# Two-layer hybrid block: residual tiles loaded ahead of the mixer-result tiles in both output projections

## The chip, the cores and the metric

The kernel runs on one core of a Trainium2 chip. The metric is the time of one execution in microseconds (us), measured on the device; lower is better. TensorE (PE) multiplies matrices, VectorE (DVE), ScalarE (ACT) and GpSimd (POOL) do elementwise work, and every DMA of this kernel is issued by SyncE (SP), whose queue issues them one after the other in the order of the program.

## The reference

Two layers of a block that runs three mixers side by side on 1024 positions of width 1024, with 256 context positions beside them. The first layer needs the context's output too, the second does not. Cut to what matters here:

```python
def hybrid_layer(x, ctx, ...):
    h  = rms_norm(x) * (1 + scale) + shift          # and hc from ctx
    ... = split_columns(h @ w_in, IN_SPLITS)
    attn_lat = attn_out(diff_attention_blocked(...), ag)
    ssd_lat  = ssd_out(ys_l, xs_l, z)               # chunked scan, both directions
    ret_lat  = ret_out(yr_l, rg)                    # retention, both directions
    mix   = concatenate([attn_lat, ssd_lat, ret_lat], axis=-1)   # 2048 wide
    x_new = x + gate * (mix @ w_out)
    ...
    ctx_new = ctx + gate_c * (mix_c @ w_out)
```

The change touches only how `mix @ w_out` and the sum with `x` are fed.

## The kernel before

Activations lie transposed, features on the 128 partitions and positions along the rows. The positions are cut into three chunks: c0 (0 to 511), c1 (512 to 1023) and c2 (the 256 of the context). Each float32 matrix product is made of three products of rounded halves: a tile `ah` and its remainder `al`, a weight `wh` and its remainder `wl`; ACT makes the rounded half, DVE or POOL the remainder (line 284).

The mixers write their results to an HBM buffer `mix` of 16 tiles of 128 features. The product with `w_out` is done in two parts. `out1` takes the eight tiles of the scan mixer as soon as those are there, adds gate times product to the residual `x` and stores the sum as `x1`; `out2` takes the other eight tiles and adds to `x1`. In both, `load_mix` brings a chunk's eight tiles by DMA (`mr`, line 1201); in `out1` DVE scales them (line 1205) before they are split. Then `out1` goes through four weight blocks of two output tiles each (`ci` 0 to 3) and, in each, through the chunks. A finished group of matmuls lies in one of two PSUM buffers. `evac` empties it: a DMA brings the residual tile `xr` (line 1221, from `in_xt` in the first layer, from `xl` in the second), DVE multiplies the PSUM tile by the gate and adds it to `xr` (line 1223), and a DMA stores the sum (line 1225). PE can begin the third group from now only when line 1223 has emptied the buffer of the first.

The tiles `mr` and `xr`, and many others, come from one pool `work` of eight buffers of 128x512 float32. A DMA into a `work` tile waits until the tile's former owner is done with it, and because the SP queue is in order, everything behind that DMA waits too.

Nobody writes the order of the instructions by hand. The code yields pieces of several such streams, and a scheduler then lays each engine's instructions out by its own estimate of times, so that retention pieces (rotations at lines 924 to 929, `ks` and `qs` at lines 1141 and 1167, `rs` at 1156, the finish of a head at lines 1090 and 1099) stand between those of `out1` on each engine. `raw` (line 270) are weight tiles. In the first layer `out2` also loads the `x1` tiles `xn` (line 469), which line 1292 updates.

Of the kernel before, what the change touches and what calls it, by code (L numbers as in the profile page):

```python
# [26 lines left out]
CHUNKS = ((0, 512), (512, 512), (1024, 256))  # L27
# [20 lines left out]
def drain(g):  # L48
    for _ in g:
        pass  # L50


class Net:
# [1156 lines left out]
    def out1(self, l, last, cols, xin):  # L1210
        nc = self.nc
        cs = (0, 1) if last else (0, 1, 2)
        for c in cs:
            self.load_mix(c, range(4, 12), cols, True)
            yield 0.5
        ada = self.ada_t[l]
        for ci in range(4):
            def evac(ft, t0, n, ps):
                f = 2 * ci + ft
                x = self.keep_x(f, t0, n) if self.mixed else self.work("xr")[:, 0:n]  # L1220
                nc.sync.dma_start(out=x, in_=xin[f, :, t0:t0 + n])
                gc = ada[:, 16 + f, 0 if t0 < LAT else 1:][:, 0:1]
                nc.vector.scalar_tensor_tensor(out=x, in0=ps, scalar=gc, in1=x, op0=ALU.mult, op1=ALU.add)  # L1223
                if not self.mixed:
                    nc.sync.dma_start(out=self.x1[f, :, t0:t0 + n], in_=x)

            w = self.next_w()
            for c in cs:
                t0, n = CHUNKS[c]
                for ft in range(2):  # L1230
                    if self.mixed and ci > 1 and len(self.wu) < 2:
                        self.stage_u(l)
                    evac(ft, t0, n, self.t_group(w, ft, c))
                    yield n * 24 / 2400
# [15 lines left out]
    def out2(self, l, last, cols, xout):  # L1250
        nc = self.nc
        while self.pieces:
            self.pieces.pop(0)()
        cs = (0, 1) if last else ORDER
        ada = self.ada_t[l]
        ws = []
        for ci in range(2):
            hi, lo = self.next_w(ci == 0)
            for ft in range(2):
                f = slice(ft * P, ft * P + P)  # L1260
                ws.append(([hi[:, k, f] for k in range(KT)], [lo[:, k, f] for k in range(KT)]))
        for pc in range(4):
            if len(self.wu) <= pc:
                self.stage_u(l)
        for hi, lo in self.wu:
            ws.append(([hi[:, k, :] for k in range(KT)], [lo[:, k, :] for k in range(KT)]))
        self.wu = []
        self.x1t = {}
        xs = {}
        for c in cs:  # L1270
            self.load_mix(c, (0, 1, 2, 3, 12, 13, 14, 15), cols, False)
            if not last:
                xs[c] = self.load_x(c, self.x1, "xn2")
        for c in cs:
            if c == cs[-1]:
                self.prefetch()
            t0, n = CHUNKS[c]
            ah, al = self.act[c]
            acc = self.work("acc") if not last else None
            for f in range(KT):  # L1280
                ps = self.pmm()
                self.mm3(ps[:, 0:n], ws[f][0], ws[f][1], [ah[:, k, :] for k in range(KT)],
                         [al[:, k, :] for k in range(KT)], True)
                if last:
                    x = self.x1k.pop((t0, f), None)
                    if x is None:
                        x = self.work("xr")[:, 0:n]
                        nc.sync.dma_start(out=x, in_=self.x1[f, :, t0:t0 + n])
                else:
                    x = xs[c][f]  # L1290
                gc = ada[:, 16 + f, 0 if c < 2 else 1:][:, 0:1]
                nc.vector.scalar_tensor_tensor(out=x, in0=ps[:, 0:n], scalar=gc, in1=x, op0=ALU.mult, op1=ALU.add)
                nc.sync.dma_start(out=xout[f, :, t0:t0 + n], in_=x)
                if not last:
                    self.sumsq_add(acc, x, f, n)
                    if c == cs[-1] and f == 3:
                        self.load_dt(l + 1)
                        self.layer_params(l + 1)
            if not last:
                def post(c=c, xs=xs[c], acc=acc):  # L1300
                    return self.norm_h(l + 1, c, xs, self.norm_r(c, acc))

                if c != cs[-1]:
                    drain(post())
                else:
                    self.posts = {0: post}
# [247 lines left out]
```

## Time and profile before

| | us |
|---|---|
| median of 3 runs | 2867.38 (2867.06 to 2869.82) |
| the profiled execution's own time | 2869.1 |
| its span, first to last instruction | 2867.3 |
| PE busy | 2665.5 (93%) |
| DVE busy | 1781.3 (62%) |
| ACT busy | 1056.4 (37%) |
| POOL busy | 772.1 (27%) |

The profiled execution is 1.7 us above the median, 1.8 us of its time lie outside the span, and PE is busy for nearly all of it. Times below are microseconds from the span's start.

### The profile page before, as it was taken

Reading aid. Unit: us, or ns where it says so; the run is one execution under the profiler, and the core shown is the slowest. Engines: PE = TensorE matmul, PEld = TensorE weight load, DVE = VectorE, ACT = ScalarE, POOL = GpSimd, SP = SyncE. Lnnn points to the kernel's source line nnn. Section 1 sums busy time; section 2 is a strip of 40 time slices with the busy share of each in tenths; the row PEclk is TensorE's granted clock in tenths of the full one; section 3 lists DMA queues with packets and bytes.
Section 4 is the critical chain, followed back from the end, with each engine's and each line's share of the span. In section 5 each row is a group of like instructions: output and inputs, shape, how many; then the busy total and the mean of one; then the engine's idle time right before and its main releaser. Section 6 shows DMA issues by size and latency. Waiting matters only on the chain.

```text
span 2867.3 us, 45100 instructions
## 1 busy us (share of the span) xinstructions
PE 2665.5 (93%) x17116; PEld 2339.0 (82%) x17116; DVE 1781.3 (62%) x4213; ACT 1056.4 (37%) x2678; POOL 772.1 (27%) x688
## 2 busy tenths in 40 slices
PE   6799999999999999989989989999999999999999
PEld 4578877888888899977878777878988888889787
DVE  5567767656677766565435566667676767564651
ACT  3443333224454545341223443332254444442330
POOL 2333223232111121243331423223421221022540
PEclk9899999999999999998999999999999999999999
DMA  6021212222111111033452112112210010002461
GB/s 244 10 62 62 67 44 83 70 69 89 45 54 45 54 31 39 27 110 109 136 179 95 36 41 72 53 50 65 60 30 16 23 30 23 23 17 66 139 209 55
DMA packets 111832, 196.04 MB, mean 68 GB/s; under 512 B 13600, under 2 KB 43104, under 8 KB 111616
## 3 DMA queue, kind: packets, MB, share of 16 engines
q1 hardware_dynamic: 111616, 193.17, 21.3%
q8 instruction: 135, 2.21, 0.3%
q14 instruction: 81, 0.66, 0.1%
HBM read 155.43 MB, written 37.68 MB: 67 GB/s over the span
## 4 chain that ended last, share of the span: by engine, by line
PE 76%; DVE 12%; ACT 3%; issue 2%; DMA 2%; POOL 1%; SPq 0%; DVEq 0%; ACTq 0%; POOLq 0%
PE mm L310 34%; PE mm L312 18%; PE t L149 5%; PE o L1037 4%; PE s L986 4%; PE s L772 2%; PE s L822 2%; DVE mx L988 2%; PE o L815 2%; PE t L793 1%; ACT e L998 1%; DVE e L1016 1%; DMA mr<-mix 1%; DVE rs L1156 1%; PE s L1146 1%
## 5 line engine op out<-in xcount | busy, mean ns | idle before, releaser
L310 PE MATMUL mm<-ah,wh 128*128 128x512 f32 (+1 forms) x1680 | 629.4, 375 | 30.1 <-DVE xr L1223 13.8
L310 PE MATMUL mm<-al,wh 128*128 128x512 f32 (+1 forms) x1680 | 622.8, 371 | 1.5 <-DVE al L284 0.9
L310 PE MATMUL mm<-ah,wl 128*128 128x512 f32 (+1 forms) x1680 | 622.4, 371 | 0.6 <-POOL wl L284 0.6
L284 POOL TENSOR_TENSOR wl<-raw,wh 128x512 fp32r<-128x512 f32 x224 | 294.5, 1335 | 769.5 <-ACT wh L282 736.9
L312 PE MATMUL mm<-wh,ah 128*128 128x256 f32 x1568 | 455.7, 291 | 9.5 <-DVE q L118 7.0
L312 PE MATMUL mm<-wl,ah 128*128 128x256 f32 x1568 | 450.4, 287 | 0.0
L312 PE MATMUL mm<-wh,al 128*128 128x256 f32 x1568 | 448.7, 286 | 0.0
L310 PEld LDWEIGHTS mm<-ah,wh 128*128 128x128 f32 x1680 | 322.3, 192 | 85.8 <-issue 13.8
L310 PEld LDWEIGHTS mm<-al,wh 128*128 128x128 f32 x1680 | 322.2, 192 | 51.1 <-issue 1.4
L310 PEld LDWEIGHTS mm<-ah,wl 128*128 128x128 f32 x1680 | 321.2, 191 | 51.2 <-POOL wl L284 1.1
L312 PEld LDWEIGHTS mm<-wh,ah 128*128 128x128 f32 x1568 | 302.5, 193 | 16.6 <-DVE q L118 7.7
L998 ACT ACTIVATE e<-s,nb 128x512 f32<-128x512 f32 (+1 forms) x384 | 231.7, 613 | 206.2 <-DVE nb L993 203.6
L312 PEld LDWEIGHTS mm<-wl,ah 128*128 128x128 f32 x1568 | 302.7, 193 | 2.4 <-POOL wl L284 0.2
L312 PEld LDWEIGHTS mm<-wh,al 128*128 128x128 f32 x1568 | 302.3, 193 | 2.2 <-issue 0.2
L988 DVE TENSOR_REDUCE mx<-s 128x1 f32<-128x512 f32 (+1 forms) x400 | 225.1, 589 | 55.4 <-PE s L986 53.2
L986 PE MATMUL s<-kT,qT 128*128 128x512 f32 (+1 forms) x800 | 215.8, 375 | 17.0 <-ACT e L998 15.5
L282 ACT ACTIVATE wh<-raw 128x512 fp32r<-128x512 f32 x224 | 130.0, 625 | 226.2 <-PE mm L310 103.9
L1037 PE MATMUL o<-v,aT 128*128 128x128 f32 x1312 | 174.9, 276 | 0.0
L986 PEld LDWEIGHTS s<-kT,qT 128*128 128x128 f32 x800 | 134.3, 193 | 41.3 <-ACT e L998 26.5
L1037 PEld LDWEIGHTS o<-v,aT 128*128 128x128 f32 x1312 | 163.8, 193 | 4.1 <-DVE v L118 0.8
L794 ACT ACTIVATE t<-t 128x512 f32<-128x512 f32 x144 | 82.2, 582 | 146.5 <-PE t L793 142.5
L766 POOL TENSOR_TENSOR xw<-xn,dtpk 128x512 f32<-128x512 f32 (+2 forms) x96 | 79.4, 838 | 208.9 <-PE s L772 93.5
(282 smaller groups left out, 4544.5 us busy)
## 6 DMA issues: line engine op xcount, KB each, us to landing
raw<-in_wi_dram SPq DMA_DIRECT2D x176, 256.0 KB
wa<-in_wa_dram SPq DMA_DIRECT2D x48, 512.0 KB
E<-cume SPq DMA_DIRECT2D x144, 128.0 KB
mr<-mix SPq DMA_DIRECT2D x64, 256.0 KB
raw<-in_wo_dram SPq DMA_DIRECT2D x32, 256.0 KB
x<-xr SPq DMA_DIRECT2D x26, 256.0 KB
mix<-cv SPq DMA_DIRECT2D x8, 640.0 KB
mix<-sg SPq DMA_DIRECT2D x8, 640.0 KB
```

What stands on the lines that cost most here:

```text
L149: self.nc.tensor.transpose(ps[:, j * P:(j + 1) * P], srcs[i + j], self.ident)
L282: nc.scalar.activation(out=hi, in_=x, func=AF.Copy)
L284: e.tensor_tensor(out=lo, in0=x, in1=hi.bitcast(F32), op=ALU.subtract)
L310: nc.tensor.matmul(ps, lhsT=w, rhs=x, start=st, stop=sp)
L312: nc.tensor.matmul(ps, lhsT=x, rhs=w, start=st, stop=sp)
L766: nc.gpsimd.tensor_tensor(out=xw, in0=xn[:, a:a + m].rearrange("p t (h e) -> p t h e", h=2), in1=self.wend[:, a:a + m, h0:h0 + 2].unsqueez ...
L772: nc.tensor.matmul(ps[:, j * P:(j + 1) * P], lhsT=bn[:, c, :], rhs=xw[:, j].rearrange("p h e -> p (h e)"), start=True, stop=True)
L794: nc.scalar.activation(out=ps, in_=ps, func=AF.Exp)
L986: nc.tensor.matmul(ps[:, 0:n], lhsT=qT[:, 2 * m + s, :], rhs=kT[m][:, t0:t0 + n], start=(s == 0), stop=(s == 1))
L988: nc.vector.tensor_reduce(out=mx[:, ci:ci + 1], in_=ps[:, 0:n], axis=AX.X, op=ALU.max, negate=len(chunks) == 1)
L998: nc.scalar.activation(out=em[:, t0:t0 + n], in_=pss[ci][:, 0:n], func=AF.Exp, bias=nb, accum_out=z[:, 3 * m + ci:3 * m + ci + 1])
L1037: nc.tensor.matmul(po[:, 0:P], lhsT=aT[j], rhs=v[:, j, :], start=(j == b0), stop=(j == NT - 1))
```

## The change

In `out1`, for c0 and c1, the residual tiles of the first weight block (f = 0 and 1) are loaded just ahead of that chunk's `load_mix`, by a helper `get_x`, and kept in a dictionary until `evac` takes them. All other residual tiles (the later weight blocks, and the context chunk c2) are loaded in `evac` as before. In `out2` of the first layer the `xn` tiles of a chunk are loaded ahead of its `load_mix` in the code. Nothing is added or removed; the sums are the same.

```diff
         cs = (0, 1) if last else (0, 1, 2)
+        early = {}
+
+        def get_x(f, t0, n):
+            x = self.keep_x(f, t0, n) if self.mixed else self.work("xr")[:, 0:n]
+            nc.sync.dma_start(out=x, in_=xin[f, :, t0:t0 + n])
+            return x
+
         for c in cs:
+            if c < 2:
+                early.update({(f, CHUNKS[c][0]): get_x(f, *CHUNKS[c]) for f in range(2)})
             self.load_mix(c, range(4, 12), cols, True)
             yield 0.5
...
                 f = 2 * ci + ft
-                x = self.keep_x(f, t0, n) if self.mixed else self.work("xr")[:, 0:n]
-                nc.sync.dma_start(out=x, in_=xin[f, :, t0:t0 + n])
+                x = early.pop((f, t0), None)
+                kept = (t0, f) in self.x1k
+                if x is None:
+                    x, kept = get_x(f, t0, n), self.mixed
...
-                if not self.mixed:
+                if not kept:
                     nc.sync.dma_start(out=self.x1[f, :, t0:t0 + n], in_=x)
...
         for c in cs:
-            self.load_mix(c, (0, 1, 2, 3, 12, 13, 14, 15), cols, False)
             if not last:
                 xs[c] = self.load_x(c, self.x1, "xn2")
+            self.load_mix(c, (0, 1, 2, 3, 12, 13, 14, 15), cols, False)
```

Line 1221 of before is line 1217 after, 1223 is 1234, 1225 is 1236, 1292 is 1303 and 1293 is 1304.

On SP, in `out1` of the first layer, this stands in the queue of the changed kernel from the last `mr` loads of c0 to the middle of those of c1 (`x_0_349` is the buffer of `x1`):

```order
L1217 DMA xr_12912<-in_xt_dram 128x512
L1217 DMA xr_12914<-in_xt_dram 128x512
L1201 DMA mr_12918<-mix_348 128x512
...
L1201 DMA mr_12963<-mix_348 128x512
L1217 DMA xr_12968<-in_xt_dram 128x512
L1217 DMA xr_12970<-in_xt_dram 128x512
L1201 DMA mr_12974<-mix_348 128x512
...
L1201 DMA mr_13014<-mix_348 128x512
L1236 DMA x_0_349<-xr_12912 128x512
L1201 DMA mr_13019<-mix_348 128x512
L1236 DMA x_0_349<-xr_12914 128x512
```

Before, the end of the same stretch was this: the last `mr` load of all three chunks, then the first residual tiles.

```order
L1201 DMA mr_13059<-mix_348 128x256
L1221 DMA xr_13099<-in_xt_dram 128x512
L1221 DMA xr_13130<-in_xt_dram 128x512
L1113 DMA retd_13134<-in_retd_dram 128x256
L1225 DMA x_0_349<-xr_13099 128x512
L1225 DMA x_0_349<-xr_13130 128x512
```

The two residual loads of c0 have moved from behind 24 `mr` loads to ahead of them, those of c1 to between the chunks, and the two stores of c0's sums now stand around c1's last `mr` load.

On DVE, at the same place, the changed kernel empties c0's first groups here (`al` is the remainder of an `mr` tile, `rO` the finish of a retention head, `mr_12999` to `mr_13019` the last four tiles of c1):

```order
L284 TENSOR_TENSOR al_12973<-mr_12984,ah_12972 128x512
L1090 TENSOR_TENSOR rO_12732<-rO_12732,ry_13165 128x512 x2
L1090 TENSOR_TENSOR rO_12732<-rO_12732,ry_13165 128x256
L1234 SCALAR_TENSOR_TENSOR xr_12912<-mm_13082,ada_148,xr_12912 128x512
L284 TENSOR_TENSOR al_12973<-mr_12994,ah_12972 128x512
L1234 SCALAR_TENSOR_TENSOR xr_12914<-mm_13111,ada_148,xr_12914 128x512
L1205 SCALAR_TENSOR_TENSOR mr_12999<-mr_12999,cols_113,s_12976 128x512
```

and before it did so here, behind the scaling of the last `mr` tile of c2 (`mr_13059`):

```order
L1205 SCALAR_TENSOR_TENSOR mr_13059<-mr_13059,cols_113,s_13043 128x256
L134 SCALAR_TENSOR_TENSOR ry_13161<-ru_13163,ry_13161 128x10
L284 TENSOR_TENSOR al_13017<-mr_13049,ah_13016 128x256
L1223 SCALAR_TENSOR_TENSOR xr_13099<-mm_13074,ada_148,xr_13099 128x512
L132 TENSOR_TENSOR ru_13163<-ry_13161 128x10
L1223 SCALAR_TENSOR_TENSOR xr_13130<-mm_13105,ada_148,xr_13130 128x512
```

The first emptying has moved ahead of the last four tiles of c1 and all of c2, and the three `rO` instructions stand ahead of it.

On SP, in `out2` of the first layer, the difference is this (`raw` a weight tile, `xn` the `x1` tiles; x2 counts equal rows, names are numbered anew):

```order
-L270 DMA raw_14338<-in_wo2b_dram 128x512
-L469 DMA xn_2565_14376<-x_0_349 128x512 x2
-L469 DMA xn_2566_14379<-x_0_349 128x512 x2
...
+L270 DMA raw_14338<-in_wo2b_dram 128x512
+L469 DMA xn_2555_14342<-x_0_349 128x512 x2
+L469 DMA xn_2556_14345<-x_0_349 128x512 x2
```

The `xn` loads of c0 stand behind the same weight tile as before, with four `mr` loads of c1 ahead of that tile in both; only the two first `xn` loads of c1 have moved, ahead of the last four `mr` loads of c1.

## Rows read from the trace of the kernel before

**Rows 1.** The page: the span, busy time by engine, and the store's DMA issues.

```profile
span 2867.3 us, 45100 instructions
PE 2665.5 (93%) x17116; PEld 2339.0 (82%) x17116; DVE 1781.3 (62%) x4213; ACT 1056.4 (37%) x2678; POOL 772.1 (27%) x688
...
mix<-sg SPq DMA_DIRECT2D x8, 640.0 KB
```

**Rows 2.** Waits of PE over 1255 to 1480: total, times, longest.

```profile
PE mm L310 <- DVE xr L1223: 12.8, 4, 11.1
PE mm L310 <- DVE xn L1292: 10.5, 1, 10.5
```

**Rows 3.** Timeline of PE, first layer, `out1`: start, duration, idle before.

```profile
1268.65 0.73 PE L310 MATMUL mm<-ah,wh 128*128 128x512 f32 x2 [1.49 <-ACT ah L282]
...
1296.35 0.77 PE L310 MATMUL mm<-ah,wh 128*128 128x512 f32 x1 [11.11 <-DVE xr L1223]
...
1325.45 0.57 PE L310 MATMUL mm<-ah,wh 128*128 128x512 f32 x1 [1.08 <-DVE xr L1223]
```

**Rows 4.** Timeline of the SP queue, first layer, `out1`.

```profile
1262.39 1.85 SPq L1201 DMA_DIRECT2D mr<-mix  x4
...
1268.35 21.29 SPq L1201 DMA_DIRECT2D mr<-mix  x20
1290.59 0.92 SPq L1221 DMA_DIRECT2D xr<-in_xt_dram  x2
...
1322.87 0.33 SPq L1104 DMA_DIRECT2D mix<-sg  x1
```

**Rows 5.** Timeline of DVE, first layer, `out1`.

```profile
1267.19 0.75 DVE L1205 SCALAR_TENSOR_TENSOR mr<-mr,cols,s 128x512 f32<-128x512 f32 x1 [3.76 <-PE o L1185]
...
1283.28 0.83 DVE L284 TENSOR_TENSOR al<-mr,ah 128x512 fp32r<-128x512 f32 x1
...
1293.76 0.47 DVE L1205 SCALAR_TENSOR_TENSOR mr<-mr,cols,s 128x256 f32<-128x256 f32 x1
...
1295.46 0.74 DVE L1223 SCALAR_TENSOR_TENSOR xr<-mm,ada,xr 128x512 f32<-128x512 f32 x1
...
1303.52 2.45 DVE L1090 TENSOR_TENSOR rO<-rO,ry 128x512 f32<-128x512 f32 x3
...
1322.36 0.48 DVE L1099 SCALAR_TENSOR_TENSOR sg<-t,gcol,sg 128x256 f32<-128x256 f32 x1
...
1324.92 0.48 DVE L1223 SCALAR_TENSOR_TENSOR xr<-mm,ada,xr 128x256 f32<-128x256 f32 x1
```

**Rows 6.** Stretches of 10 us: busy time (count) by engine, PE's granted clock, DMA.

```profile
1270.00:1280.00 10.00, 9.99 (x44) 8.51 (x45) 10.00 (x16) 6.66 (x20) 3.87 (x3) 0.83 0.77 256
1280.00:1290.00 10.00, 5.24 (x28) 4.27 (x26) 10.00 (x20) 5.79 (x12) 6.51 (x5) 0.91 0.53 158
1290.00:1300.00 10.00, 3.65 (x9) 2.94 (x10) 10.00 (x16) 2.00 (x5) 8.11 (x7) 0.50 0.46 147
1300.00:1310.00 10.00, 10.00 (x46) 8.27 (x45) 9.18 (x18) 0.60 (x1) 4.82 (x9) 0.91 0.19 69
```

**Rows 7.** Timeline of the SP queue, first layer, `out2`.

```profile
1448.83 0.33 SPq L270 DMA_DIRECT2D raw<-in_wo2b_dram  x1
1449.21 9.47 SPq L469 DMA_DIRECT2D xn<-x  x15
```

**Rows 8.** Waits of PE over 2640 to 2867: second layer, both projections.

```profile
PE o L1184 <- DVE rw L1176: 2.4, 1, 2.4
PE s L1146 <- POOL ks L1141: 1.0, 1, 1.0
PE mm L310 <- DVE xr L1223: 0.9, 1, 0.9
PE t L149 <- POOL qs L1167: 0.8, 1, 0.8
```

**Rows 9.** Stretches of 10 us in the second layer, `out1`.

```profile
2660.00:2670.00 10.00, 6.81 (x35) 5.22 (x34) 9.72 (x14) 5.36 (x10) 7.57 (x7) 1.00 0.58 178
2670.00:2680.00 10.00, 9.94 (x44) 8.63 (x45) 7.93 (x12) 2.06 (x9) 6.38 (x6) 0.83 0.55 180
```

## The prediction

> **What bounds the kernel now.** I read the page first, for the engine that carries the span: PE is busy for 2665.5 of 2867.3 us [rows 1], so only work that makes PE idle, or slow, can be won, some 200 us in all. Then I read the waits of PE around each place that the change touches, for the wait that ends last there, and the timelines of SP and DVE for what that wait itself waited for.
>
> In the first layer's first projection PE stands idle for 11.11 us before 1296.35, and what ends it is the emptying of c0's first group [rows 2, 3]. PE had thus finished c0 at 1296.35 - 11.11 = 1285.24. The emptying ran at 1295.46 for 0.74 us [rows 5], and PE went on 0.15 us after its end. Why so late? Its residual tile was asked for at 1290.59, because the SP queue was held by twenty `mr` loads from 1268.35 for 21.29 us, 1.06 us each [rows 4]. And DVE, which takes its instructions in order, was busy for all of 1270 to 1300 [rows 6] and had the emptying behind the scaling of c2's last `mr` tile at 1293.76 [rows 5]. So there are two reasons, a load that comes late and a place in DVE's order that comes late; the two order listings of the change show that both have been moved up. After the gap PE's granted clock is 0.50 in 1290 to 1300, which is the lower of its two levels (1.2 GHz), and 0.91 as a mean of 1300 to 1310 [rows 6]. That loses half of the 3.65 us that PE was busy there and 9% of the next ten, 1.8 + 0.9 = 2.7 us.
>
> In the first layer's second projection PE waits 10.5 us for the first emptying there [rows 2], whose `xn` loads are issued from 1449.21 on, right behind a weight tile at 1448.83 [rows 7].
>
> In the second layer's two projections together PE waits only 0.9 us for a residual [rows 8]. There the pause of c0 is filled by retention work of the pair before; PE's idle time in 2660 to 2670 is 10 - 6.81 = 3.2 us [rows 9], and the waits that account for it are for `rw` (2.4) and `qs` (0.8) [rows 8], not for a residual tile.
>
> **The change, part by part.**
>
> *First layer, `out1`, c0 and c1.* No DMA and no instruction is added. The price is in the order. Two loads of 256 KB now stand ahead of c0's tiles and two more ahead of c1's, and they hold two, then four, of the eight `work` buffers. At 1.06 us for a place in the queue, c0's tiles come up to 2.1 us later and c1's up to 4.2 us; if the buffers do not bind, nothing.
>
> The first emptying on DVE stands behind the remainder of c1's second tile and three `rO` instructions. Before, that remainder ended at 1283.28 + 0.83 = 1284.11, and the three `rO` take 2.45 us [rows 5]. With the emptying's 0.74 and the 0.15 us to PE this gives 1287.45 if the `mr` loads are not delayed, and 1291.65 if c1's come the whole 4.2 us later. Before it was 1296.35. So c1 begins 4.7 to 8.9 us earlier; I take the middle, 6.8. (The lower bound from PE is 1285.24, when c0 ends, which is below both.) c0's own later tiles cost nothing in this sum as long as c0 ends before about 1288, since DVE's place is later; that is the cover, and if c0 were to end 2.1 us later (1287.3) it would still just hold.
>
> What then comes late is the next meeting point, the first matmul of the second weight block, at 1325.45 before, which waits for c2's first emptying at 1324.92 [rows 3, 5]. c2's residual tiles are not loaded early. In the changed queue they stand behind the store of a retention result, which before was issued at 1322.87, as soon as its last piece ended at 1322.36 + 0.48 = 1322.84 [rows 4, 5]. That store moves up with PE, by the same 6.8 us, but the residual load can only go 0.33 us behind it and then has to land. No row shows how long that load takes by itself. Bounds: the bytes alone, 128 KB at the 256 GB/s of the best stretch [rows 6], are 0.5 us; from the issue of the first `mr` at 1262.39 to its use at 1267.19 are 4.8 us [rows 4, 5]. I take 3.8, near the upper end, since a store of 640 KB [rows 1] goes right ahead of it. Then the block begins at 1323.20 + 3.8 + 0.48 + 0.05 = 1327.53 on the old scale, 2.1 us later than 1325.45; with 0.5 us nothing is lost, with 4.8 it is 3.1. So 6.8 - 2.1 = 4.7 us stay, with bounds of 4.7 - 3.1 = 1.6 and 8.9.
>
> The Trainium skill, DMA: Bandwidth & Descriptors, section Anatomy of one DMA, fits a fixed part of about 2.0 us plus bytes over 436 GB/s, measured on another issue path than the one used here; my estimate from it is 2.3 us for this load. By that figure 0.6 us would be lost in place of 2.1, and the gain would be 6.2 us; no row here isolates it.
>
> *The clock.* If a gap of 2 to 6 us is left, PE's clock falls again: after PE's short waits at the beginning of c0, of which the longest is 1.49 us [rows 3], the stretch 1270 to 1280 has a mean of 0.83 [rows 6], a loss of 1.7 us, where the long gap lost 2.7. I count 0.3 of the 1.0 us between them, with bounds of 0 and, if the gap disappears, 2.7.
>
> *First layer, `out2`.* In the code the `xn` loads go ahead of `mr`; in the built order c0's stand behind the same weight tile as before, with the same `mr` loads ahead of it. What made PE wait 10.5 us is where it was. I count 0, with bounds of -1 and +1 for the shift of two loads of c1 past four `mr` loads (0.63 us each, 9.47/15 [rows 7]).
>
> *Second layer, `out1`.* The residual was not waited for, so there is nothing to win from the load itself. What the moved emptying could win is at most the 3.2 us of idle time and the 17% that the clock lacks in the next ten, 1.7 us [rows 9], 4.9 in all. What it can lose: two stores of `x1` come between c1's last `mr` loads, and behind those DVE has the `rw` of the last retention group, for which PE waits already [rows 8]; one wait for a store and a load is again up to 4.8 us. I take 0 between +4.9 and -4.8. Between the projections the scheduler has also reordered pieces of the scan, where PE hardly waits; I count 0 there, which is an assumption.
>
> Sum: 4.7 + 0.3 + 0 + 0 = 5.0 us less. The profiled execution had 2869.1 us, so it would have had 2864.1; it stood 1.7 us above the median of 2867.4. Against the median the forecast is **2862.4 us**.
>
> **The rivals.**
>
> *The whole gap goes.* PE wins 11.1 + 2.7 = 13.8 us and no later wait takes it back: 2853.6. For it: both reasons of the wait are removed, and c1 can begin at 1285.24 if DVE is early. Against it: DVE was busy for every one of the 30 us around it [rows 6], so the emptying cannot come before the work that still stands ahead of it, and c2's residual is not early. Chance 0.15. With it I put the cases in which 8 to 12 us are won.
>
> *Given back, or not given at all.* The start of c1 is earlier, but c2's residual load, behind its store, or a wait within c1 or c2 takes the gain back by 1325.45; 2867, within 2 us. The second half of the change is of that kind already, a move in the code that the built order does not show. For it: the 1.08 us wait before 1325.45 is already for that emptying [rows 3]. Against it: the store moves up with PE. Chance 0.25.
>
> *Slower: too few `work` buffers.* Residual tiles that lie idle until their group is done hold four of eight buffers while the `mr` tiles pass through the other four. c1's last tile waits for a store of a residual that was itself just emptied: from 1291.65 a store (4.8 by the bound), a load (4.8), then scaling, rounding and remainder (0.75 and 0.83 [rows 5], and the rounding between them taken as long as the scaling, 2.3), 1303.6 us. PE wants that tile after 21 of c1's first 24 matmuls, at the half clock of 0.41 us (3.65/9 [rows 6]) 1291.65 + 8.6 = 1300.3. That is a wait of 3.3 us, and c2's first two tiles wait for the other stores in the same way, another 3.3. It decides when these waits exceed the 4.7 us gained at the start of c1 together with the 3.1 that the late c2 load can cost: 4.7 - 3.1 - 6.6 = -5.0 us, and the same pattern in the second layer adds up to 4.8. I put it between the two, at 2874. Against it: DVE and POOL freed `mr` tiles at 1.06 us each with eight buffers, and much of that pace was DVE's. Chance 0.12.
>
> **How the numbers follow.** The forecast has 0.48, the whole gap 0.15, given back 0.25, slower 0.12. The forecast's own range is 2858 to 2867 (gains of 1.6 to 8.9, rounded outward). A change of 0.2%, 5.7 us, is about what a measurement of this kernel can tell from none, so 2861.7 and 2873.1 are the borders. Of the forecast's 0.48 I put 0.2 below 2861.7, which with 0.15 and nothing of the other two gives 0.36 for faster (0.35 and a little of the reordered middle); of the slow case 0.08 lies above 2873.1. The rest is 0.56. The range of 2855 to 2872 leaves out most of the whole-gap case and the worse half of the slow one, some 0.18.
>
> **What would show it.** The idle time before c1's first matmul falls from 11.1 us to between 2 and 7, with DVE's emptying as releaser still, and c1 begins between 1287 and 1292 if the span's scale holds up to there. The second weight block begins 2 to 8 us earlier than 1325.45, and waits for c2's emptying, whose load is issued right behind the `sg` store. In `out2` the wait for `xn` stays at 10 us or so. In the second layer the wait for `rw` moves, and the sum of PE's waits from 2640 on stays within 5 us of before. I would be wrong if PE shows new waits for `ah` or `al` within c1 or c2, if the `xn` wait is gone, or if the middle of the second layer has moved by more than the first layer's gain.

## The result and the profile after

The changed kernel takes 2890.94 us (median of 5 runs, 2889.22 to 2895.42) where the kernel before takes 2867.38 (5 runs): a ratio of 1.0076, with a 95% interval of 1.0062 to 1.0089. It is slower by 0.8%, 21.8 us by the ratio (the medians are 23.6 apart); the forecast was 2862.4, and the range ended at 2872.

The page of the changed kernel, to be read against [rows 1]:

```profile
span 2889.4 us, 45094 instructions
PE 2681.2 (93%) x17116; PEld 2348.5 (81%) x17116; DVE 1783.1 (62%) x4213; ACT 1057.4 (37%) x2678; POOL 769.2 (27%) x688
```

PE does the same 17116 matmuls in 15.7 us more of busy time and has 6.4 us more of idle time (2889.4 - 2681.2 = 208.2 against 201.8), so the loss is not one pause. To find its places I compared when the n-th matmul of each source line starts in the two traces, and took the median difference over 12 us to either side of a few points. In the table each column is how much that difference grows within a stage, in us. The points are times of the first profile of before: the first layer's `out1` lies in 1235 to 1400, its `out2` in 1400 to 1465, a part of the second layer's scan that proved to matter in 1600 to 1850, the second layer's `out1` in 2640 to 2762; "other" is 1465 to 1600 and 1850 to 2640. The last two columns say how long the queue took for all `mr` loads of `out1`, from the first issue to the end of the last, in each layer.

| kernel | ratio | out1, layer 1 | out2 | scan 1600-1850 | other | out1, layer 2 | mr, layer 1 | mr, layer 2 |
|---|---|---|---|---|---|---|---|---|
| before | 1 | 0 | 0 | 0 | 0 | 0 | 27.2 | 19.3 |
| before, second profile | - | -0.8 | +1.6 | +1.0 | +1.0 | -2.7 | | |
| the change | 1.0076 | +3.5 | +1.4 | +4.1 | +1.5 | +10.6 | 37.1 | 28.9 |
| e1 out2 only | 1.0002 | -0.4 | 0.0 | +3.1 | +0.2 | -0.6 | | |
| e2 out1 only | 1.0077 | +3.6 | +2.0 | +4.2 | +0.4 | +7.9 | 36.2 | 28.2 |
| e3 first layer | 1.0039 | +2.6 | -0.6 | +5.4 | +1.7 | +0.7 | 35.7 | 19.2 |
| the same, second profile | - | +3.8 | +1.6 | +4.2 | +0.8 | -0.1 | | |
| e4 second layer | 1.0040 | -0.1 | +1.8 | +1.0 | +4.6 | +10.8 | 27.2 | 29.2 |
| e5 other pool | 0.9985 | -4.5 | +2.7 | +3.9 | -5.1 | -1.5 | 31.0 | 20.2 |
| e6 behind the chunk | 1.0035 | -1.0 | +1.8 | +4.1 | +1.1 | +0.5 | 32.7 | 23.5 |
| e7 other pool, first layer | 0.9978 | -2.9 | +1.9 | +3.5 | -5.8 | -2.6 | 31.1 | 19.6 |
| e8 c0 behind | 0.9978 | -3.6 | +1.9 | +3.4 | -9.8 | +0.4 | 29.7 | 23.2 |
| e9 hold | 1.0075 | +8.0 | -0.5 | +3.8 | -2.4 | +10.8 | 37.3 | 28.5 |
| e10 layout | 0.9987 | -2.8 | -8.6 | +5.3 | +1.8 | -1.1 | 27.1 | 22.6 |
| e11 c0 ahead | 1.0027 | -0.6 | +2.1 | +5.0 | -0.1 | +2.4 | 31.0 | 21.2 |
| e12 c0, first layer | 0.9972 | -3.6 | -0.6 | +5.6 | -8.4 | -0.1 | 29.7 | 19.3 |

The second row is the noise of one profile against another of the same program: 1 to 3 us in a stage. Two other rows show noise too: up to 2640 every engine of e4 has the order of before, and PE, DVE and POOL of e1 have it throughout, and still e1 shows +3.1 in the scan and e4 +4.6 in "other". The stretch before 1235, where before and after have the same order, is not in the table; it scatters from -1.4 to +9.2 us between these profiles, so spans of single profiles say little and ratios over several runs are given.

*First layer, `out1`.* PE's timeline of the changed kernel, the starts that follow an idle time, against [rows 3]:

```profile
1272.08 0.79 PE L1184 MATMUL o<-rv,rw 128*128 128x128 f32 x2 [3.86 <-DVE rO L118]
1288.16 0.71 PE L426 MATMUL s<-ident,rg 128*128 128x128 f32 x4 [1.07 <-DVE mr L1205]
1292.12 0.58 PE L310 MATMUL mm<-ah,wh 128*128 128x512 f32 x1 [3.25 <-DVE xr L1234]
1309.33 1.08 PE L149 MATMUL t<-ident,rk 128*128 128x128 f32 x4 [4.48 <-DVE rk L929]
...
1324.75 0.71 PE L1146 MATMUL s<-rv,ks 128*128 128x128 f32 x4 [2.13 <-POOL ks L1141]
...
1330.78 0.80 PE L310 MATMUL mm<-ah,wh 128*128 128x512 f32 x1 [0.24 <-DVE xr L1234]
```

The pause ahead of c1 is indeed 3.25 us in place of 11.11, and c1 begins at 1292.12, 5.3 us earlier than before (1296.35, plus the 1.06 us by which this trace runs late at that point). Yet three other long pauses have appeared, one ahead of c0's groups and two behind c1, and the second weight block begins at 1330.78, which is 4.3 us later than before by the same count. The SP queue shows the first reason, against [rows 4]:

```profile
1263.45 0.90 SPq L1217 DMA_DIRECT2D xr<-in_xt_dram  x2
1264.40 0.90 SPq L1201 DMA_DIRECT2D mr<-mix  x2
...
1269.50 6.05 SPq L1201 DMA_DIRECT2D mr<-mix  x6
1277.95 2.32 SPq L1217 DMA_DIRECT2D xr<-in_xt_dram  x2
1280.36 9.81 SPq L1201 DMA_DIRECT2D mr<-mix  x7
1292.01 0.32 SPq L1236 DMA_DIRECT2D x<-xr  x1
1292.60 0.32 SPq L1201 DMA_DIRECT2D mr<-mix  x1
...
1294.07 7.40 SPq L1201 DMA_DIRECT2D mr<-mix  x8
...
1324.43 0.38 SPq L1104 DMA_DIRECT2D mix<-sg  x1
1324.86 2.56 SPq L1217 DMA_DIRECT2D xr<-in_xt_dram  x3
```

The 24 `mr` loads end at 1301.47, 37.1 us after the first; before it was 27.2 [rows 4]. c2's residual is issued 0.43 us behind the issue of the `sg` store, as foreseen. DVE's timeline, against [rows 5]:

```profile
1263.80 0.69 DVE L118 COPY rO<-o 128x512 f32<-128x512 f32 x1 [0.86 <-PE o L1185]
1270.67 0.75 DVE L1205 SCALAR_TENSOR_TENSOR mr<-mr,cols,s 128x512 f32<-128x512 f32 x1 [6.19 <-DMA mr<-mix]
1271.34 0.68 DVE L118 COPY rO<-o 128x512 f32<-128x512 f32 x1
...
1291.24 0.74 DVE L1234 SCALAR_TENSOR_TENSOR xr<-mm,ada,xr 128x512 f32<-128x512 f32 x1
```

DVE waits 6.19 us for the first `mr` tile, which is now behind two residual tiles in the queue, and the copy of a retention result stands behind it in DVE's order; PE waits for that copy, 3.86 us. In the same way the rotations `rk` come after the late `mr` tiles of c2, and PE waits 4.48 us for them.

The two projections as a whole, windows of before and then of after (busy time and count by engine, PE's granted clock, DMA share):

```profile
1250.00:1350.00 100.00, 85.69 (x492) 74.33 (x491) 68.53 (x128) 29.94 (x74) 40.02 (x44) 0.90 0.42 135
2640.00:2790.00 150.00, 144.12 (x757) 121.35 (x756) 96.62 (x171) 50.48 (x122) 76.83 (x71) 0.99 0.54 171
```

```profile
1250.00:1350.00 100.00, 84.45 (x475) 73.35 (x474) 67.58 (x126) 29.95 (x74) 40.15 (x44) 0.91 0.42 131
2640.00:2790.00 150.00, 139.31 (x715) 115.90 (x714) 88.31 (x173) 43.20 (x110) 61.43 (x67) 0.95 0.45 142
```

In the first layer PE is idle for 15.55 us in place of 14.31: the long pause has been cut into pieces, not removed. The mean granted clock is 0.91 against 0.90, so of the 3.5 us of the table some 1.2 are idle time, and the clock does not show where the rest went. In the second layer it is idle for 10.69 in place of 5.88, and the mean granted clock is 0.95 in place of 0.99, 6 us of 150; 4.8 + 6 is about the 10.6 us of the table. In that layer the `mr` tiles were nearly always on time before, and are not now. The group of their scalings on DVE in 2635 to 2715, with what ended the idle time ahead of them, of before and of after:

```profile
L1205 DVE SCALAR_TENSOR_TENSOR mr<-mr,cols,s 128x512 f32<-128x512 f32 x16 | 11.3, 740 | 5.4 <-PE s L426 4.4 <-DMA mr<-mix 1.0
```

```profile
L1205 DVE SCALAR_TENSOR_TENSOR mr<-mr,cols,s 128x512 f32<-128x512 f32 x16 | 11.8, 747 | 13.4 <-DMA mr<-mix 13.4
```

DVE waits 13.4 us for these loads where it waited 1.0; its idle time ahead of them is 13.4 us in all against 5.4. PE's longest waits there are now these, against [rows 8]:

```profile
PE mm L310 <- DVE xr L1234: 4.2, 3, 2.5
PE t L149 <- DVE rO L1090: 3.8, 2, 2.4
```

And this is what the `mr` loads themselves waited for in the SP queue of the second layer (total, times, longest), before (2644 to 2666):

```profile
SPq L1201 <- DVE al L284: 4.1, 3, 1.7
SPq L1201 <- POOL al L284: 2.2, 4, 0.7
```

and after (2655 to 2688):

```profile
SPq L1201 <- DVE al L284: 5.9, 5, 1.6
SPq L1201 <- POOL al L284: 5.2, 3, 3.2
SPq L1201 <- DMA x<-xr: 2.7, 1, 2.7
```

A load waits until an older tile has been split into its halves (`al`), 11.1 us in place of 6.3, and once for the store of an early residual tile, a wait that was not there before.

### The profile page after: what moved, and what is told of

Read it like the earlier page. It is cut to its first block, busy times and chain, and to the rows that moved or that the text cites. A ratio compares the mean times of both kernels' runs of the same rounds, so it can differ in the third digit from the quotient of the medians.

```text
span 2889.4 us, 45094 instructions
## 1 busy us (share of the span) xinstructions
PE 2681.2 (93%) x17116; PEld 2348.5 (81%) x17116; DVE 1783.1 (62%) x4213; ACT 1057.4 (37%) x2678; POOL 769.2 (27%) x688
## 4 chain that ended last, share of the span: by engine, by line
PE 74%; DVE 13%; DMA 3%; ACT 3%; issue 2%; POOL 1%; SPq 0%; DVEq 0%; ACTq 0%; POOLq 0%
PE mm L310 33%; PE mm L312 17%; PE t L149 5%; PE s L986 4%; PE o L1037 4%; PE s L822 2%; PE s L772 2%; DVE mx L988 2%; PE o L815 1%; DMA mr<-mix 1%; PE t L793 1%; ACT e L998 1%; DVE rs L1156 1%; DVE e L1016 1%; DMA raw<-in_wi_dram 1%
## 5 line engine op out<-in xcount | busy, mean ns | idle before, releaser
L310 PE MATMUL mm<-ah,wh 128*128 128x512 f32 (+1 forms) x1680 | 634.3, 378 | 24.6 <-DVE xn L1303 10.6
```

The source lines that it names most:

```text
L310: nc.tensor.matmul(ps, lhsT=w, rhs=x, start=st, stop=sp)
```

## The experiments

The theories. *Buffers*: a residual tile that is loaded early keeps one of the eight `work` buffers until its group is done; the `mr` tiles pass through those that are left, their loads come more slowly, and what stands behind them in the order of each engine comes late. *Place*: 256 KB loads ahead of the `mr` loads, or the earlier place of the emptying on DVE, cost. *Layout*: any change lets the scheduler lay out the code behind it anew, and the new order costs. "Before" ran 18 to 30 times beside these kernels; each ratio's interval is in brackets.

**The two halves and the two layers apart.** e1 makes only the edit in `out2`, e2 only that in `out1`, e3 and e4 only that in `out1` of the first and of the second layer (the diff is e3's; e4 has `last` for `not last`):

```diff
-            if c < 2:
+            if c < 2 and not last:
                 early.update({(f, CHUNKS[c][0]): get_x(f, *CHUNKS[c]) for f in range(2)})
```

> Only the second projection of the first layer is changed (xn loads ahead of mr in the code), the first projection is that of before. Buffer theory (the residual tiles take work buffers from the mr tiles in the first projection): no loss here, 2867 within 3 us, and the first projections of both layers take as long as before. Layout theory (any change of the code lets the scheduler lay out everything behind it anew, and that new order is what costs): the second layer's middle and its first projection move here too, so a loss of 5 to 15 us, 2872 to 2882, all of it behind the second projection.

> Only the first projections are changed, in both layers; the second projection is that of before. Buffer theory: nearly the whole loss stays, 2886 to 2893, with about 3.5 us lost in the first layer's first projection and about 10 us in the second layer's. Layout theory: the loss is of another size, since the second layer is laid out anew by another starting point; anything between 2868 and 2895, and not the same 10 us at the second layer's first projection.

> The early residual loads in the first layer's first projection alone. Buffer theory: 3 to 4 us lost there, and nothing at the second layer's first projection, so 2870 to 2873. Layout theory: the 3 to 4 us and besides them a loss behind that, in the scan of the second layer and in its first projection, so 2878 or more.

> The early residual loads in the second layer's first projection alone; everything before it is that of before. Buffer theory: the 10 us that the change lost there are lost here too, 2875 to 2880. Layout theory: less than half of it, 2867 to 2872, since the order there depended on what came before.

Measured: e1 2871.34 against 2870.85 us, 1.0002 (0.9994 to 1.0011); e2 2893.41, 1.0077 (1.0059 to 1.0095); e3 2880.09, 1.0039 (1.0025 to 1.0053); e4 2880.73, 1.0040 (1.0025 to 1.0056). `out2` does nothing, `out1` is the whole loss, and the layers add up. The expected times were counted from 2867, and before stood some 3.5 us higher in these rounds, so the differences are compared: 0.5, 22.6 and 9.9 us in e1, e2 and e4 are what the buffer theory asks for. e3 is a miss of it: 9 to 11 us in place of 3 to 6, and as a total near what the layout theory asked for. Its own stage shows 2.6 and the scan behind it, whose code is that of before, 5.4; the second layer's projection, where the layout theory wanted a loss too, shows 0.7.

**The same loads into other buffers, or behind the chunk.** e5 keeps the place of the loads, but takes one buffer of the pool `unit` for the two residual tiles of a chunk; e7 does so in the first layer alone. e6 keeps the `work` buffers and loads behind the chunk's `mr` tiles; e8 does so for c0 only.

```diff
-                early.update({(f, CHUNKS[c][0]): get_x(f, *CHUNKS[c]) for f in range(2)})
+                xe = self.unit("xe", (P, 2, 512))
+                for f in range(2):
+                    early[f, CHUNKS[c][0]] = xe[:, f, :]
+                    nc.sync.dma_start(out=xe[:, f, :], in_=xin[f, :, CHUNKS[c][0]:CHUNKS[c][0] + 512])
```

> The first projections of the change, but the early residual tiles lie in buffers of the other pool (unit, one buffer for the two tiles of a chunk), so that the mr tiles have all eight work buffers. The loads keep their place in the code ahead of the chunk's mr loads. Buffer theory: the loss of both first projections goes, and the pause of 11.1 us in the first layer stays short, so 2855 to 2865. Rival (the bytes ahead of mr, or the new order of the elementwise work, cost and not the buffers): 2880 to 2893 as in the change.

> The first projections of the change, with the early residual tiles in work buffers as in the change, but loaded behind the chunk's own eight mr loads in place of ahead of them. Buffer theory: c0's tiles start as early as before, but c1's tiles still share the work buffers with two residual tiles, so half of the loss goes, 2873 to 2882. Rival (place in the queue alone costs): the loss goes, 2862 to 2868.

> As the kernel with the residual tiles in the other pool, in the first layer's first projection alone; the second layer's code is that of before. Buffer theory: the gain of the short pause, 2857 to 2864. Rival (no gain is to be had there): 2866 to 2872.

> Early residual tiles of c0 alone, in work buffers, loaded behind c0's own mr loads; those of c1 as before. Two buffers in place of four are held, and c0's mr loads aren't delayed. Buffer theory: less than a third of the loss of the change, 2865 to 2874. Rival (the place of the emptying in DVE's order costs): 2878 or more.

Measured (before 2870.96): e5 2867.52, 0.9985 (0.9974 to 0.9996); e6 2880.65, 1.0035 (1.0022 to 1.0048); e7 2864.41, 0.9978 (0.9967 to 0.9988); e8 2863.33, 0.9978 (0.9968 to 0.9988). With the same loads at the same place in the code and the `work` buffers free, the loss of both projections is gone: -4.5 and -1.5 us in place of +3.5 and +10.6. (As differences from before all four lie in the buffer theory's ranges but e8, which is better than its range.) The built order is not quite that of the change. This is e5's queue in the first layer (line 1225 loads the residual tiles `xe`):

```profile
1264.01 0.90 SPq L1225 DMA_DIRECT2D xe<-in_xt_dram  x2
1264.95 1.87 SPq L1201 DMA_DIRECT2D mr<-mix  x4
1267.17 1.59 SPq L1225 DMA_DIRECT2D xe<-in_xt_dram  x2
```

All four residual tiles are loaded as early as in the change or earlier, so in the first layer a later load cannot be what takes the loss away. In the second layer c0's two stand behind six `mr` loads, where the change has them ahead of all, and c1's two behind seven in place of eight. DVE's wait for `mr` in the second layer, e5:

```profile
L1205 DVE SCALAR_TENSOR_TENSOR mr<-mr,cols,s 128x512 f32<-128x512 f32 x16 | 11.4, 741 | 6.3 <-PE s L426 4.4 <-DMA mr<-mix 1.7
```

1.7 us, not 13.4, and 6.3 in all; no `mr` load waits for a residual's store. The place is not free: in the first layer the queue still needs 31.0 us for the `mr` loads, and PE waits there for the copy behind the first `mr` tile as in the change (3.48 us; 3.65 in e7), and for c1's operands where it waited for the emptying. The starts in e5's timeline:

```profile
1272.26 0.59 PE L1184 MATMUL o<-rv,rw 128*128 128x128 f32 x2 [3.48 <-DVE rO L118]
1292.50 0.47 PE L310 MATMUL mm<-ah,wh 128*128 128x512 f32 x1 [4.71 <-ACT ah L282]
```

e6 is unclear by itself. Its ratio fell where the buffer theory put it, but its two projections show -1.0 and +0.5 us, so its loss lies elsewhere, in the scan and in scatter that one profile does not resolve. It holds `work` buffers too, but takes them behind the chunk's loads, and its trains of 32.7 and 23.5 us cost the projections nothing that the table shows.

**Buffers held, loads meant to stay.** e9 takes the buffers where the change does, but loads one column of 128 into each; the whole tile was meant to come at the emptying, as before.

```diff
-                early.update({(f, CHUNKS[c][0]): get_x(f, *CHUNKS[c]) for f in range(2)})
+                for f in range(2):
+                    x = early[f, CHUNKS[c][0]] = self.work("xr")
+                    nc.sync.dma_start(out=x[:, 0:1], in_=xin[f, :, CHUNKS[c][0]:CHUNKS[c][0] + 1])
...
+                else:
+                    nc.sync.dma_start(out=x, in_=xin[f, :, t0:t0 + n])
```

> The first projections take the four work buffers at the places where the change does, but only one column of each residual tile (a 128x1 piece) is loaded there; the whole tile is loaded at the emptying, as in the kernel before. So buffers are held and no bytes and no emptying move ahead. Buffer theory: the mr loads of the first layer stretch from 27 us to about 36 and those of the second from 19 to about 28, as in the change, and the loss is at least that of the change, 2885 to 2905. Rival (the 256 KB loads ahead of the mr loads, or the early emptying's place on DVE, cost): the trains stay at 27 and 19 us within 3, and 2866 to 2876.

Measured: 2892.29 against 2871.27 us, 1.0075 (1.0055 to 1.0096), the change's own loss. The queue and DVE's wait of e9:

```profile
1267.16 0.90 SPq L1224 DMA_DIRECT2D xr<-in_xt_dram  x2
1268.10 0.90 SPq L1201 DMA_DIRECT2D mr<-mix  x2
1270.19 1.53 SPq L1236 DMA_DIRECT2D xr<-in_xt_dram  x2
...
1283.31 1.53 SPq L1236 DMA_DIRECT2D xr<-in_xt_dram  x2
...
1295.74 9.66 SPq L1201 DMA_DIRECT2D mr<-mix  x11
```

```profile
L1205 DVE SCALAR_TENSOR_TENSOR mr<-mr,cols,s 128x512 f32<-128x512 f32 x16 | 11.7, 745 | 14.7 <-DMA mr<-mix 10.2 <-PE s L426 4.4
```

37.3 us from the first to the last `mr` load, and 10.2 us of waiting for them in the second layer. But the loads did not stay: line 1224 loads the column, line 1236 the whole tile, and the scheduler has put the whole tiles of c0 behind only the first two `mr` loads and those of c1 right behind their columns; in the second layer c0's stand behind three `mr` loads, at 2661.36. So e9 does not have the buffers without the loads, as its expectation says. It shows that the loss does not need the residual loads ahead of the very first `mr` tiles: the 3.86 us ahead of the copy are gone there, and the loss is not.

What parts buffers from loads is e5, and e11 below for the second layer. There e11 has c0's two tiles ahead of all `mr` loads, in `work` buffers, and shows +2.4 us; the change adds c1's two behind eight `mr` loads and shows +10.6; e5 loads c1's two behind seven, into other buffers, and shows -1.5. So the larger part of that loss goes with the buffers, not with the place. (In the first layer e9 loses more than the change, +8.0 against +3.5; why is not shown.)

**The layout alone, and fewer buffers.** e10 is the kernel before with one number changed, a yield's weight from 0.5 to 1.0, which changes nothing but the scheduler's order (and by it one 128 KB tile of c2, which now stays on the chip, so that one store and one load drop out). e11 and e12 load for c0 alone: e11 ahead of c0's `mr` loads in both layers, e12 behind them and in the first layer only.

```diff
-            yield 0.5
+            yield 1.0
```

> The kernel before, with no load moved; only the weight of a yield in the first projections is 1.0 in place of 0.5, so that the scheduler lays out the code behind it anew. It measures what a new layout alone does. If layout scatter is small: 2868 to 2874 and no stage moves by more than 2 us. If layout scatter explains the parts of the other runs that lie in the middle of the second layer (from -6 to +7 us there): the middle moves here by several us as well, in either direction, 2862 to 2885.

> Early residual tiles of c0 alone, in work buffers, loaded ahead of c0's own mr loads as in the change; c1's as before. Two buffers are held from the start in place of four. Buffer theory: the trains of mr loads are between those of before and of the change (29 to 33 us and 21 to 25), and the loss of the two first projections is less than half, 2866 to 2878. Rival (the place ahead of c0's mr loads costs, whatever is held): 2880 to 2892.

> Early residual tiles of c0 alone, in the first layer alone, in work buffers behind c0's own mr loads: the version that should beat the kernel before. The pause of 11.1 us shortens to 3 or 4, the first layer's first projection gains 3 to 4 us, and the second layer's code is that of before: 2863 to 2868 against about 2871 for the kernel before on this chip, if the new layout behind it costs nothing.

Measured (before 2871.27): e10 2867.31, 0.9987 (0.9974 to 0.9999); e11 2878.23, 1.0027 (1.0015 to 1.0039); e12 2863.16, 0.9972 (0.9959 to 0.9985). e10's total hides large parts of both signs: +5.3 us in the scan, and -8.6 in `out2`, where PE's wait for `xn` is 7.6 us in its trace in place of 10.5 [rows 2]. The +5.3 answers e3 in part: in every kernel whose first-layer `out1` or its order differs, 410 to 460 of the some 1340 matmuls of 1600 to 1850 have changed places on PE, and the stretch is 3.4 to 5.6 us longer, whatever the change does; where the order is that of before it is 1.0 (before again, e4) and 3.1 (e1). So 1 to 3 us of it are scatter. The same stretch of before, of the change and of e10, each between the same two points of the program:

```profile
1600.00:1850.00 250.00, 235.33 (x1339) 197.59 (x1338) 160.86 (x405) 94.15 (x182) 72.41 (x75) 0.96 0.18 53
```

```profile
1606.50:1860.60 254.10, 238.23 (x1335) 199.15 (x1334) 160.25 (x404) 93.97 (x182) 72.44 (x75) 0.95 0.18 52
```

```profile
1597.20:1852.50 255.30, 239.37 (x1339) 199.01 (x1338) 160.92 (x405) 94.30 (x182) 72.48 (x75) 0.95 0.18 52
```

Idle time makes 1.2 us of the difference (14.7 before, 15.9 in both others); the rest is the same matmuls taking longer, at a mean granted clock of 0.95 in place of 0.96. e11, two buffers held from the start, lies between before and the change in the lengths of both trains of loads and in the second layer's `out1` (+2.4); in the first layer's it shows no loss, and 5.0 us of its total stand in the scan. e12 has the lowest ratio here, though not clear of e7 and e8. Its stage gains 3.6 us; but its trace also shows -8.4 us in the second layer's "other" stretch, where 573 matmuls have changed places on PE, and those are not the residual's.

Over all kernels, the trains and the losses go together: where the first layer's train took 35.7 us or more its `out1` lost 2.6 to 8.0 us, and where it took 32.7 or less none was lost; in the second layer the trains of 28.2 us or more lost 7.9 to 10.8, and those up to 23.5 at most 2.4.

**The same again.** Two kernels were profiled a second time, to tell layout from scatter.

> The kernel before, unchanged, profiled a second time. If the scatter of executions is small (layout theory for the middle): the time from the end of the first layer's second projection to the start of the second layer's first projection agrees with the first profile within 1.5 us, and so does each projection. If scatter makes up the middle: it moves by 3 us or more with the same code.

> The kernel with early loads in the first layer alone, profiled a second time. Layout theory: its middle is again 5 to 9 us longer than before's, with the same waits of PE in it. Scatter: anything from 0 to 5.

Measured, one time each beside a before of 2872.44: 2878.40 and 2879.76 us. Before's middle (1465 to 2640) moved by 2.0 us, between the two bounds, and e3's was +5.0 after +7.0. Single stages of before again moved by up to 2.7, more than the 1.5 that the first bound allows. So the 4 to 5 us at 1600 to 1850 repeat with the order; single figures below some 3 us in the table, in the long "other" stretch below some 5, do not stand out.

## Why the prediction was wrong

*What bounds the kernel* held, and so did the reasons for the pause: the late load and the late place on DVE. *The start of c1* held: 4.7 to 8.9 us earlier was forecast, 5.3 was measured, with the emptying as releaser. *`out2`* held: 0, with 10.6 us of waiting for `xn` in place of 10.5; e1 shows it. *The late residual of c2* held in its order (0.43 us behind the `sg` store), but not in its time: "That store moves up with PE, by the same 6.8 us" was wrong, for the store was issued at 1324.43, 0.5 us later than before (1322.87 plus the 1.06 us), and the second weight block began 4.3 us later where 2 to 8 earlier was forecast. PE then waited for the residual only 0.24 us, because retention work was late by more. Of the signs of being wrong that I had named, one came: the middle of the second layer moved by 5.6 us, more than the gain forecast. The others did not: the first layer's new waits are not for `ah` or `al`, and the `xn` wait stayed. The sign that PE's waits from 2640 on stay within 5 us of before held, for idle time grew by 4.8 there; it did not see the clock.

The step that failed is the price of the buffers: "At 1.06 us for a place in the queue, c0's tiles come up to 2.1 us later and c1's up to 4.2 us; if the buffers do not bind, nothing." I counted the residual tiles as places, a fixed delay once. With the places alone, in e5, the first layer's train grows by 3.8 us, near the 4.2. With `work` buffers held the loads go at the pace at which buffers come free: 27.2 to 37.1 us in the first layer and 19.3 to 28.9 in the second, 10 us each, where e5 has 31.0 and 20.2. With it two terms failed:

- First layer, `out1`: "4.7 us stay" was +3.5 us lost. "The cover" that I named, c0 ending before 1288, was looked for at the matmuls only; the late first `mr` tile held back what stands behind it on DVE, a copy (3.86 us of PE's time), and late `mr` tiles of c2 held back the rotations (4.48). Neither pause alone makes the loss. The copy's belongs to the place, not to the buffers: it is 3.48 in e5, 3.65 in e7 and 3.49 in e11, and absent where two or more `mr` loads go first (e6, e8, e9, e12); e5 and e7 gain with it. The rotations' is 4.36 in e8 and 4.37 in e12, which gain too; there PE came early, and the rotations, counted from 1235, were ready at 1303.9, where they are at 1308.2 in the change (PE took them at 1304.7 before). The change has both pauses, and 2.13 us more for `ks`. The sum of PE's idle time did not fall, and each of the new pauses is followed by matmuls at the lower clock: the granted clock is 0.86 in 1310 to 1320 and 0.83 in 1330 to 1340, both 1.00 before, while the 0.50 behind the long pause is gone; the two balance, as the mean above shows. Some 2.3 of the 3.5 us stay unexplained.
- Second layer, `out1`: "I take 0 between +4.9 and -4.8" was 10.6 us lost (10.8 in e4, alone). The rows said that nothing was to be won there, and I set the price of a loss at one wait for a store and a load; the wait for a store is there, 2.7 us, but the loss was a slower train, 13.4 us of DVE's waiting, and a clock of 0.95 in place of 0.99.

The third term, "I count 0 there, which is an assumption", for the pieces that the scheduler reorders, was 4.1 us lost at 1600 to 1850; e10 and e3 show layout there, and the rows of unchanged order show that 1 to 3 us of it can be scatter. Which of the moved pieces makes it was not tried.

The rival "too few `work` buffers" named this mechanism and its condition. Its 5.0 us for the first layer are near the 3.5 measured; its 4.8 for the second are less than half of the 10.6, because it counted single waits for a store in place of the pace of all loads, and it then took a value between, 2874, and put 0.12 on it. With 3.5 + 10.6 in the projections and 4.1 in the scan, 18.2 of the 22.1 us between the two profiles are located; the rest, 1.1 before 1235 and 2.9 in `out2` and the other stretches, does not stand out of the scatter.

## What to carry to other kernels

Moving a load ahead in a program lengthens the life of its tile. Ask first which pool the tile is from, how many buffers are left to the stream that it goes ahead of, and what that stream's pace is then; a tile that waits long for its use belongs into buffers which that stream does not use, or behind the stream. Where one scheduler lays out the whole program, look in the built order whether a load stands where the code puts it: e9's did not. There a local edit also shifts stages that it does not touch by some microseconds either way, so a gain or a loss has to be seen in its own stage before it is put down to the edit.

## What the runs showed that I had not expected

Two profiles of the very same kernel differ by 9.2 us at 1235 of 2867 and agree to 1 to 3 us within each later stage; in these two the scatter lies mostly in the first half. And a change of order without a load moved in the code (e10) was worth -8.6 us in one stage and +5.3 in another (of which 1 to 3 can be scatter), nearly as much as the pause of 11.1 us that the change was about.
